# Moving the mask, the first two bias runs and half of the key copies of a neighbourhood-attention stage, with first scores two parts later

## The chip, the cores and the metric

The kernel runs on one core of one Trainium2 chip. The time is device microseconds (us) of one execution. The kernel before was timed in three runs: 1579.85, 1583.55 and 1585.72 us, median 1583.55 us. The profile used below is of one further execution of the same program.

A core has engines that run at the same time, each with its own ordered list of instructions: TensorE (PE in the profile; PEld is its loading of the stationary operand), VectorE (DVE), ScalarE (ACT), GpSimd (POOL) and SyncE (SP). SP computes nothing here: it issues DMA transfers. ACT issues transfers too, between its own computations; an instruction that has to wait holds up all that stand behind it on the same engine. In the profile, "SPq" and "ACTq" mark the issuing of a transfer.

## What is computed

The reference is one step of a small diffusion trunk of two layers, 512 latent tokens (8 rows of 64 columns) and 128 context tokens, width 1024, 16 heads of 64. The change lies in the first layer, whose token mixer is neighbourhood attention:

```
q, k, v = split(h @ w_qkv, 3)
s_lat = einsum(q, k[neighbouring rows]) * scale
s_lat = where(col_ok, s_lat + rpb[:, dr, dc], -inf)   # 2-D relative bias per head
s_ctx = einsum(q, k_ctx) * scale
p = softmax(concat(s_lat, s_ctx))
o = p_lat @ v + p_ctx @ v_ctx
```

A query of a latent token sees 16 neighbouring columns in all 8 rows, plus the 128 cached context keys. The context tokens attend only to themselves. After the mixer follow a projection, norms and a gated feed-forward block with a width-3 convolution; the second layer has grouped-query attention and the same feed-forward block. None of that is changed.

## The kernel before, in words

Weights arrive in f32. Each piece of 128x1024 is split into a high part, rounded to the matmul type (`wh`, by ACT, line 171), and the rest (`wl`, by VectorE or GpSimd, line 173); a product is three matmuls, high by high, high by low and low by high (`wsplit`, lines 166 to 180). The raw pieces `wr` are loaded by SP (line 169) into four buffers.

The beginning, up to about 52 us, loads and norms the tokens, makes the modulation and the transposed input `hT` (lines 580 to 582: ACT writes the high part, VectorE updates `xT` in place and then writes the low part), and computes the values of the first four heads (`v_part`; their copies out of PSUM are `na_v_put`, line 473). Its tiles lie in a pool that is given back at its end; the tiles of the attention stage (pool `na`, opened at line 760) are laid into the same memory, in the order of their first use, and an instruction that writes such a tile waits until the last reader of the old tile that lay there is done.

The attention stage works in pairs of heads. `na_qk_items(p)` gives for pair `p` two items: the queries and the keys, each of eight parts (two column halves, QKH, of four parts; a part is six matmuls, 128x256 in the first half and 128x384 in the second). When a half is complete, its result goes from PSUM to SBUF: for queries by lines 843 and 844, for keys by `k_put` (lines 813 to 818). `k_put` writes for each head `b` of the pair three things: the rounded key in the head's own half of the partitions (line 816, ACT), the same in the other half, "swapped" (line 817, ACT), and the rest `kl` (line 818, VectorE). The keys of the cached context come through a transpose (`tk`) and go the same way.

`na_table(h)` (lines 885 to 898) makes the bias table of a head: three transfers issued by ACT bring runs of the bias table from DRAM into the tile `tr` (one buffer; 128 rows of 996 bytes and two times 64 rows), and GpSimd subtracts them from the mask in three instructions (line 894) into one of two tiles `tb`. The mask itself is one transfer of 256 KB, issued by ACT at line 762. A second head's runs can only be fetched when the first head's table is done, because `tr` has one buffer.

`Head.scores(slot)` computes 128 queries against their 384 keys: two matmuls, VectorE adds the table and takes the minimum (line 929), ACT takes the exponential and its sum (line 933), VectorE the reciprocal (936), GpSimd scales (937). `turns` transposes the probabilities (`tp`), `values` multiplies with the values.

The order of the matmuls is written out by hand: `pe` (line 110) chains every TensorE instruction to the one before it, so TensorE works strictly in program order. `stream()` hands out the parts of all projections one by one through `fill`. At the start of the stage `fill(PRO)` takes PRO = 20 of them (16 of the first pair, 4 of the second pair's queries), then come the four score slots of head 0 with one part after each of the first three, and then, head by head, the lists ORDER0, ORDER and ORDER2, in which "f" is one more part, "s0" to "s3" are score slots of the next head and "t0" to "t2" are transposes. In all there are 173 such parts; after head 11 four early parts of the output projection (three matmuls of 128x512 each, `part0`) are put behind them, and head 12 uses up what is left.

On the other engines the order is not written out: a planner at build time lists instructions, by what it takes them to cost and to wait for. `behind(a, b)` (line 707) tells it that `a` has to stand after `b`; it adds no wait. There is one counter of completions for every eighth transfer, over both queues together, so that a transfer also waits for the one eight before it.

ACT keeps one table of functions at a time; the profile shows the loading of another one as ACT_TABLE_LOAD. The first of the stage's exponentials stands behind such a load.

Of the kernel before, what the change touches and what calls it, by code (L numbers as in the profile page):

```python
# [10 lines left out]
F32 = mybir.dt.float32  # L11
F32R = mybir.dt.float32r
BF16 = mybir.dt.bfloat16
AF = mybir.ActivationFunctionType
# [5 lines left out]
P = 128  # L20
D = 1024
# [13 lines left out]
RPAD = 32  # L35
RLEN = 15 * 31 + 2 * RPAD
RUN = 8 * 31 + 1
# [3 lines left out]
NPK = 6  # L41
# [14 lines left out]
    "t0 s0 s1 f f f t1 f f t2 f s2 f s3 f f f f f f f".split(),  # L56
    "p0 s0 s1 t0 f f f t1 f t2 f s2 p1 f s3 v p2 f f f f".split(),
)
PRO = 20
PSTEP = (3, 5, 6, 6, 8, 9)  # L60
WU = 29
TP = 1
# [10 lines left out]
def raw_ap(ap, offset, dims):  # L73
    return bass.AP(tensor=ap.tensor, offset=ap.offset + offset, ap=[list(d) for d in dims])
# [30 lines left out]
def hybrid_step(ctx: ExitStack, tc: tile.TileContext, A, O):  # L105
    nc = tc.nc
    no_sync = mybir.DependencyInfo(mybir.DependencyClass.NoSync, mybir.DependencyReason.DATA)
# [11 lines left out]
    def turn(*a, **k):  # L119
        pe(nc.tensor.transpose(*a, **k))  # L120

    def f32(t):
        return t.bitcast(F32)

# [37 lines left out]
    def x_in(t):  # L162
        return A["x_sample"][0, t * P : (t + 1) * P, :] if t < 4 else A["x_prompt"][0]


    def wsplit(src, a, b, low=None, own=None, pin=False, after=None):
        q = own or wp
        raw = wp.tile([P, a, b], F32, tag="wr", name="wr")
        nc.sync.dma_start(raw, src)
        hi = q.tile([P, a, b], F32R, tag="wh", name="wh")  # L170
        i = nc.scalar.copy(hi, raw)  # L171
        lo = q.tile([P, a, b], F32R, tag="wl", name="wl")
        j = (low or nc.vector).tensor_sub(lo, raw, f32(hi))  # L173
        if after:
            behind(i, after[0])
            behind(j, after[1])
        if pin:
            tc.keep_in_program_order(i)
            tc.keep_in_program_order(j)
        return hi, lo  # L180

    def rows(w, r0, nr, c0, ncol):
        return w[r0 * P : (r0 + nr) * P, c0 : c0 + ncol].rearrange("(k p) n -> p k n", p=P)
# [81 lines left out]
    def ada_work(p, rawp, group, steps, todo, wait=1, sizes=()):  # L265

        bias = p.tile([P, 256], F32, name="abias")
        gr = p.tile([P, 256], F32, name="again")  # L270
        nc.gpsimd.memset(bias, 0.0)
        nc.gpsimd.memset(gr, 0.0)

        def quarters(row):
            return row.rearrange("(j c) -> j c", j=4)

        loads = deque((l, idx, k) for l, idx in todo for k in range(KC))
        raws = deque()

        def load():  # L280
            if loads:
                l, idx, k = loads.popleft()
                raw = rawp.tile([P, D], F32, tag="wr", name="wr")
                nc.sync.dma_start(raw, A["ada_w"][l, k * P : k * P + P, idx * D : idx * D + D])
                raws.append((l, idx, k, raw))

        for _ in range(group):
            load()
        for _ in range(wait):
            yield  # L290
        sizes = iter(sizes)
        while raws:
            n = min(len(raws), next(sizes, len(raws)))
            for _ in range(n):
                l, idx, k, raw = raws.popleft()
                if k == 0:
                    for q in range(2):
                        nc.sync.dma_start(bias[q::32, :], quarters(A["ada_b"][l, idx * D : idx * D + D]))
                        if idx in gain_of:
                            nc.sync.dma_start(gr[q::32, :], quarters(A[gain_of[idx]][l]))  # L300
                    ps = bk.get("ada")
                for j in range(4):
                    mm(ps[32 * j : 32 * j + 32, 0:256], scolp[:, 2 * k : 2 * k + 32], raw[:, 256 * j : 256 * j + 256],
                       start=k == 0, stop=k == KC - 1)
                if k < KC - 1:
                    continue
                orow = p.tile([P, 256], F32, tag="arow", name="arow")
                nc.vector.tensor_add(orow, ps[:, 0:256], bias)
                bk.put(ps)
                if idx in gain_of:  # L310
                    nc.vector.scalar_tensor_tensor(
                        orow, orow, 1.0 if idx in (1, 4) else 0.0, gr, op0=ALU.add, op1=ALU.mult
                    )
                for q in range(2):
                    nc.scalar.dma_start(quarters(modrow[l][idx][q]), orow[q::32, :])
            for i in range(steps):
                for _ in range(n if steps == 1 else i < n):
                    load()
                yield
# [150 lines left out]
        return vpool.tile([P, 6, 4, HD], F32, tag="vt", name="vt", bufs=2)  # L470

    def na_v_put(vt, c, src):
        nc.scalar.copy(vt[:, c], src.rearrange("p (a d) -> p a d", a=4))

    def na_v_cache(vts, g):
        vc = vpool.tile([P, 256], F32, tag="vc", name="vc", bufs=1)
# [13 lines left out]
    with ExitStack() as s:  # L490
# [154 lines left out]
        v_part(6, range(NT))  # L645
        for c in range(NT):
            v_part(7, (c,))
            na_v_put(vts_of[0], c, vb[c][:, 0:256])
            if c == 4:
                na_v_out(0, vb[c][:, 0:256])  # L650
            bk.put(vb[c])

# [49 lines left out]
            nc.scalar.copy(hi, raw)  # L704
            return nc.vector.tensor_sub(lo, raw, f32(hi))

    def behind(ins, other):
        tc.add_manual_dep(ins.ins, other.ins.name, no_sync, reason="order")

    class Mix:  # L710


# [46 lines left out]
    with l_na:  # L759
        ap = l_na.enter_context(pool("na", 2))  # L760
        mask = ap.tile([P, 2, 32, 8], F32, name="mask", bufs=1)
        nc.scalar.dma_start(mask, A["k_mask"])
        tbs = [ap.tile([P, 7, P], F32, name=f"tb{i}", bufs=1) for i in range(2)]
        for tb in tbs:
            nc.gpsimd.memset(tb[:, 3, :], 0.0)
# [33 lines left out]
        def na_qk_items(p):  # L799
            d = {}  # L800
# [8 lines left out]

            def load_k():  # L810
                d["wk"] = wsplit(rows(wqkv, 0, 8, 1024 + P * p, P), 8, P, nc.gpsimd if p else None)

            def k_put(c0, c1, src):
                for b in range(2):
                    own, oth = own_oth(b)
                    nc.scalar.copy(d["kh"][b][own, c0:c1], src[own])
                    nc.scalar.copy(d["kh"][b][oth, c0:c1], src[own])
                    nc.vector.tensor_sub(d["kl"][b][own, c0:c1], src[own], f32(d["kh"][b][own, c0:c1]))

            def part(which, half, k0):  # L820
                w = d["w"] if which == 0 else d["wk"]
# [61 lines left out]
            return v6[:, 0:5:2, :] if slot == 0 else v6[:, slot - 1 : slot + 2, :]  # L883

        def na_table(h):
            tr = ap.tile([P, 2, RUN], F32, tag="tr", name="tr", bufs=1)
            base = h * RLEN + RPAD
            for dst, off, n in ((tr[:, 0, :], -8, 16), (tr[0:64, 1, :], 8, 8), (tr[64:128, 1, :], -16, 8)):
                nc.scalar.dma_start(dst, raw_ap(A["k_rpb"], base + off, [[1, n], [31, 8], [1, RUN]]))
            tb = tbs[h % 2]  # L890
            for w, dst in ((1, tb[:, 0::6, :]), (0, tb[:, 1:3, :]), (0, tb[:, 4:6, :])):
                t0 = tr[:, w, :]
                rv = raw_ap(t0, RUN - 1, [t0.ap[0], [-16, 2], [-1, 16], [-31, 8]])
                nc.gpsimd.tensor_sub(
                    dst.rearrange("p c (a b) -> p c a b", b=8),
                    mask[:, w].rearrange("p (c a) b -> p c a b", c=2), rv,
                )
            return tb
# [983 lines left out]
```

## Time and profile before

| | |
|---|---|
| median of three runs | 1583.55 us (1579.85 to 1585.72) |
| profiled execution, its own time | 1582.82 us |
| span of the profiled execution, first to last instruction | 1580.9 us |
| TensorE busy in the span | 1524.0 us, 96% |
| VectorE, ACT, GpSimd busy | 1024.6, 861.1, 701.9 us |
| mean granted TensorE clock | 0.99 |

The page of a profile and the views behind it name instructions by line, engine, operation and tile, as `out<-in`. In a view of the timeline each row gives the start, the duration, the engine, the line and the operation; in square brackets stands how long the engine was idle before it and what released it. A row of stages gives start and end, the length, the busy time of PE, PEld, DVE, ACT and POOL, the granted TensorE clock (1.00 is full) and the share of the DMA engines' time. The idle time of an engine costs something only where it ends up on the path that sets the end.

### The profile page before, as it was taken

How to read it: one execution, taken by the hardware profiler on the slowest of the kernel's cores; microseconds unless marked ns; L12 is line 12 of the kernel's file. 1: busy time of each engine (PE TensorE's matmuls, PEld its weight loads, DVE VectorE, ACT ScalarE, POOL GpSimd, SP SyncE). 2: the span in 40 equal slices, each digit the busy share in tenths (PEclk: the TensorE clock that was granted, in tenths of full speed). 3: DMA queues.
4: the chain of work that ended last, by engine and by line, in shares of the span. 5: the costliest groups of instructions: out<-in, count | busy, mean ns of one | idle time of the engine just before them, and what ended most of it. 6: DMA issues, size and time to landing. Idle time of an engine off the chain costs nothing.

```text
span 1580.9 us, 26049 instructions
## 1 busy us (share of the span) xinstructions
PE 1524.0 (96%) x9709; PEld 1349.4 (85%) x9709; DVE 1024.6 (65%) x1654; ACT 861.1 (54%) x1641; POOL 701.9 (44%) x605
## 2 busy tenths in 40 slices
PE   6799999999999999999999989999999999999998
PEld 4689899788999999988887767777899999998886
DVE  4353444649877666765746867773888888886554
ACT  4474655646655555554444536764656666554443
POOL 1455554332355455534443354541325556553433
PEclk9999999999999999999999998999999999999999
DMA  9845454244465666587573110003633334448664
GB/s 300 196 113 142 127 145 118 75 151 157 154 231 185 218 186 201 176 272 267 192 223 112 60 39 15 1 1 131 229 116 105 114 105 150 132 157 269 213 217 140
DMA packets 193210, 242.41 MB, mean 153 GB/s; under 512 B 11100, under 2 KB 149564, under 8 KB 193084
## 3 DMA queue, kind: packets, MB, share of 16 engines
q1 hardware_dynamic: 182224, 233.13, 46.0%
q10 hardware_dynamic: 10860, 7.62, 2.9%
q8 instruction: 76, 1.25, 0.3%
q14 instruction: 50, 0.41, 0.1%
HBM read 214.38 MB, written 26.34 MB: 152 GB/s over the span
## 4 chain that ended last, share of the span: by engine, by line
PE 58%; DVE 7%; ACT 3%; POOL 3%; issue 2%; DMA 2%; ACTq 0%; POOLq 0%; DVEq 0%
PE ux L117 17%; PE acc L117 16%; PE uz L117 8%; PE uy L117 4%; PE y L117 2%; PE po L117 2%; PE s L117 2%; PE gp L117 2%; PE tp L120 2%; PE ada L117 2%; DVE t L1244 1%; DMA wr<-in_ffn_w_up 1%; DMA wr<-in_ffn_w_down 1%; DVE wl L173 1%; POOL wl L173 1%
## 5 line engine op out<-in xcount | busy, mean ns | idle before, releaser
L173 POOL TENSOR_TENSOR wl<-wr,wh 128x1024 fp32r<-128x1024 f32 x70 | 172.2, 2464 | 237.4 <-ACT wh L171 226.5
L1167 POOL TENSOR_TENSOR wl<-wr,wh 128x1024 fp32r<-128x1024 f32 x76 | 183.5, 2436 | 47.3 <-ACT wh L1166 43.8
L117 PE MATMUL ux<-B,wh 128*128 128x322 f32 x832 | 200.0, 311 | 0.0
L1244 DVE SCALAR_TENSOR_TENSOR t<-C,cw,t 128x644 f32<-128x644 f32 x176 | 156.3, 888 | 51.3 <-ACT t L1242 50.7
L117 PE MATMUL acc<-wh,alo 128*128 128x512 f32 x440 | 172.3, 392 | 0.3 <-DVE alo L1136 0.3
L117 PE MATMUL acc<-wl,ahi 128*128 128x512 f32 x440 | 172.0, 391 | 0.3 <-POOL wl L173 0.3
L117 PE MATMUL acc<-wh,ahi 128*128 128x512 f32 x440 | 171.9, 391 | 0.0
L171 ACT CAST wh<-wr 128x1024 fp32r<-128x1024 f32 x140 | 145.0, 1048 | 45.1 <-DMA wr<-in_ffn_w_down 33.6
L117 PE MATMUL uz<-B,wh 128*128 128x322 f32 x640 | 156.3, 312 | 0.0
L117 PEld LDWEIGHTS ux<-B,wh 128*128 128x128 f32 x832 | 143.6, 189 | 2.1 <-issue 1.2
L1136 DVE TENSOR_TENSOR alo<-ain,ahi 128x384 fp32r<-128x384 f32 (+1 forms) x88 | 79.5, 923 | 87.7 <-ACT ahi L1134 86.7
L117 PE MATMUL ux<-B,wl 128*128 128x322 f32 x416 | 129.5, 311 | 2.7 <-DVE wl L1167 2.7
L117 PE MATMUL qk<-hT,wh 128*128 128x384 f32 (+1 forms) x512 | 123.4, 317 | 0.0
L117 PEld LDWEIGHTS uz<-B,wh 128*128 128x128 f32 x640 | 110.9, 189 | 3.7 <-issue 1.6
L1167 POOL TENSOR_TENSOR vl<-wr,vh 128x1024 fp32r<-128x1024 f32 x38 | 96.5, 2540 | 24.6 <-ACT vh L1166 24.3
L173 DVE TENSOR_TENSOR wl<-wr,wh 128x1024 fp32r<-128x1024 f32 x70 | 93.7, 1352 | 20.0 <-ACT wh L171 19.5
L1166 ACT CAST wh<-wr 128x1024 fp32r<-128x1024 f32 x84 | 84.9, 1049 | 39.3 <-DVE wr L1190 39.0
L1242 ACT ACTIVATE t<-C,cw 128x644 f32<-128x644 f32 x88 | 78.6, 893 | 47.9 <-DVE C L1272 40.3
L117 PE MATMUL uz<-B,wl 128*128 128x322 f32 x320 | 99.5, 311 | 0.3 <-POOL wl L1167 0.3
L117 PEld LDWEIGHTS acc<-wh,alo 128*128 128x128 f32 x440 | 82.6, 188 | 18.9 <-DVE alo L1136 1.1
L117 PEld LDWEIGHTS acc<-wl,ahi 128*128 128x128 f32 x440 | 82.6, 188 | 18.5 <-POOL wl L173 0.7
L117 PEld LDWEIGHTS acc<-wh,ahi 128*128 128x128 f32 x440 | 82.6, 188 | 17.7
(251 smaller groups left out, 3885.2 us busy)
## 6 DMA issues: line engine op xcount, KB each, us to landing
wr<-in_ffn_w_up SPq DMA_DIRECT2D x88, 512.0 KB
wr<-in_ffn_w_down SPq DMA_DIRECT2D x88, 512.0 KB
wr<-in_ada_w SPq DMA_DIRECT2D x80, 512.0 KB
act<-act SPq DMA_DIRECT2D x44, 321.0 KB
wr<-in_na_w_qkv SPq DMA_DIRECT2D x24, 512.0 KB
mod<-modrow SPq DMA_DIRECT2D x20, 512.0 KB
ain<-act SPq DMA_DIRECT2D x44, 192.0 KB
wf<-in_ada_w SPq DMA_DIRECT2D x16, 512.0 KB
```

The costliest lines, as they stand in the source:

```text
L117: pe(nc.tensor.matmul(*a, **k))
L120: pe(nc.tensor.transpose(*a, **k))
L171: i = nc.scalar.copy(hi, raw)
L173: j = (low or nc.vector).tensor_sub(lo, raw, f32(hi))
L1136: pin(nc.vector.tensor_sub(lo[:, 0 : c1 - c0], ain[:, 0 : c1 - c0], f32(hi[:, 0 : c1 - c0])))
L1166: nc.scalar.copy(hl[0], src)
L1167: low.tensor_sub(hl[1], src, f32(hl[0]))
L1242: nc.scalar.activation(t, taps(0), AF.Identity, bias=cw[:, 3, n : n + 1], scale=cw[:, 1, n : n + 1])
L1244: nc.vector.scalar_tensor_tensor(t, taps(d), cw[:, w, n : n + 1], t, op0=ALU.mult, op1=ALU.add)
```

## The change

- The mask and the runs of heads 0 and 1 are issued by SP instead of ACT, directly behind the load of the first pair's key weights (`load_k`). The runs of head 1 get a buffer of their own, out of the six of tag `pk`.
- The three loads by SP that follow in program order (`queue.extend([i] * 3)`; these are the weights of the second pair's queries and keys and the first piece of the modulation weights `ada_w`) are put behind the last of those transfers.
- The runs of head 2 stay in ACT's list; they are put behind the last copy of the first pair's keys by ACT (`kput`).
- The swapped key halves of the first pair (line 817) are written by VectorE instead of ACT.
- A small exponential of one column stands behind the last value copy of the first stage, so that the table of functions is loaded there.
- PRO goes from 20 to 22: two more parts run ahead of head 0's scores.

`behind` moves up in the file without a change. The diff:

```diff
-PRO = 20
+PRO = 22
...
+    queue = []
...
     def wsplit(src, a, b, low=None, own=None, pin=False, after=None):
         q = own or wp
         raw = wp.tile([P, a, b], F32, tag="wr", name="wr")
-        nc.sync.dma_start(raw, src)
+        i = nc.sync.dma_start(raw, src)
+        if queue:
+            behind(i, queue.pop())
...
                 raw = rawp.tile([P, D], F32, tag="wr", name="wr")
-                nc.sync.dma_start(raw, A["ada_w"][l, k * P : k * P + P, idx * D : idx * D + D])
+                i = nc.sync.dma_start(raw, A["ada_w"][l, k * P : k * P + P, idx * D : idx * D + D])
+                if queue:
+                    behind(i, queue.pop())
...
     def na_v_put(vt, c, src):
-        nc.scalar.copy(vt[:, c], src.rearrange("p (a d) -> p a d", a=4))
+        return nc.scalar.copy(vt[:, c], src.rearrange("p (a d) -> p a d", a=4))
...
-            na_v_put(vts_of[0], c, vb[c][:, 0:256])
+            i = na_v_put(vts_of[0], c, vb[c][:, 0:256])
...
+        behind(nc.scalar.activation(sm.tile([P, 1], F32, name="exp1"), mhalf, AF.Exp), i)
...
         mask = ap.tile([P, 2, 32, 8], F32, name="mask", bufs=1)
-        nc.scalar.dma_start(mask, A["k_mask"])
+        runs, kput = {}, []
+
+        def na_runs(h, q=nc.scalar):
+            if h == 1:
+                tr = ap.tile([P, 512], F32, tag="pk", name="tr1", bufs=NPK)[:, 0 : 2 * RUN]
+                tr = tr.rearrange("p (a b) -> p a b", a=2)
+            else:
+                tr = ap.tile([P, 2, RUN], F32, tag="tr", name="tr", bufs=1)
+            runs[h] = tr
+            base = h * RLEN + RPAD
+            for dst, off, n in ((tr[:, 0, :], -8, 16), (tr[0:64, 1, :], 8, 8), (tr[64:128, 1, :], -16, 8)):
+                i = q.dma_start(dst, raw_ap(A["k_rpb"], base + off, [[1, n], [31, 8], [1, RUN]]))
+                if h == 2:
+                    behind(i, kput[0])
+            return i
...
             def load_k():
                 d["wk"] = wsplit(rows(wqkv, 0, 8, 1024 + P * p, P), 8, P, nc.gpsimd if p else None)
+                if not p:
+                    nc.sync.dma_start(mask, A["k_mask"])
+                    for h in range(2):
+                        i = na_runs(h, nc.sync)
+                    queue.extend([i] * 3)
...
                     own, oth = own_oth(b)
-                    nc.scalar.copy(d["kh"][b][own, c0:c1], src[own])
-                    nc.scalar.copy(d["kh"][b][oth, c0:c1], src[own])
+                    i = nc.scalar.copy(d["kh"][b][own, c0:c1], src[own])
+                    (nc.scalar.copy if p else nc.vector.tensor_copy)(d["kh"][b][oth, c0:c1], src[own])
                     nc.vector.tensor_sub(d["kl"][b][own, c0:c1], src[own], f32(d["kh"][b][own, c0:c1]))
+                if not p:
+                    kput[:] = [i]
...
         def na_table(h):
-            tr = ap.tile([P, 2, RUN], F32, tag="tr", name="tr", bufs=1)
-            base = h * RLEN + RPAD
-            for dst, off, n in ((tr[:, 0, :], -8, 16), (tr[0:64, 1, :], 8, 8), (tr[64:128, 1, :], -16, 8)):
-                nc.scalar.dma_start(dst, raw_ap(A["k_rpb"], base + off, [[1, n], [31, 8], [1, RUN]]))
+            if h not in runs:
+                na_runs(h)
+            tr = runs.pop(h)
```

More of the change, by code (lines that the diff above doesn't have):

```diff
@@ L120, in turn, with behind @@
         pe(nc.tensor.transpose(*a, **k))
+    def behind(ins, other):
+        tc.add_manual_dep(ins.ins, other.ins.name, no_sync, reason="order")
     def f32(t):
@@ L705, in split @@
             return nc.vector.tensor_sub(lo, raw, f32(hi))
-    def behind(ins, other):
-        tc.add_manual_dep(ins.ins, other.ins.name, no_sync, reason="order")
     class Mix:
```

## The prediction

> **What bounds the kernel now.** I read the page first, then the timeline of TensorE for its longest idle time, then a table of stages around it, then the timelines of the engines that it points to.
>
> ```profile
> span 1580.9 us, 26049 instructions
> PE 1524.0 (96%) x9709; PEld 1349.4 (85%) x9709; DVE 1024.6 (65%) x1654; ACT 861.1 (54%) x1641; POOL 701.9 (44%) x605
> ...
> 69.47 0.28 PE L117 MATMUL qk<-hT,wl 128*128 128x256 f32 x1
> 69.59 0.28 PE L117 MATMUL qk<-hT,wh 128*128 128x256 f32 x1
> 79.36 0.69 PE L117 MATMUL s<-kh,qs 128*128 128x384 f32 x1 [9.49 <-ACT kh L817]
> ...
> 60.00:69.90 9.90, 9.87 (x72) 9.66 (x70) 1.11 (x2) 1.91 (x3) 2.79 (x4) 1.00 0.64 145
> 69.90:79.30 9.40, 0.00 (x0) 0.00 (x0) 1.87 (x6) 4.35 (x14) 4.59 (x4) 0.70 0.61 99
> 79.40:83.80 4.40, 4.40 (x13) 4.01 (x14) 2.47 (x6) 4.29 (x8) 3.20 (x2) 0.50 0.17 26
> 83.90:90.00 6.10, 6.08 (x41) 5.85 (x40) 3.14 (x13) 4.54 (x12) 4.77 (x7) 1.00 0.37 107
> ...
> 100.00:280.00 180.00, 179.25 (x1414) 162.89 (x1414) 75.75 (x227) 104.81 (x288) 93.84 (x96) 1.00 0.50 130
> 280.00:310.00 30.00, 27.97 (x185) 24.10 (x182) 20.82 (x52) 21.42 (x56) 13.52 (x15) 1.00 0.25 64
> ```
>
> TensorE is busy for 96% of the span, and its order is fixed, so each of its holes costs its whole length. One hole stands out: part 20 is done at 69.87, and the first score matmul starts at 79.36, after 9.49 us without any matmul, waiting for a swapped key half (line 817). The rows of stages show a second price: from 79.40 to 83.80 the granted clock is 0.50. It is 1.00 again in the row from 83.90. So 4.4 us of matmuls take twice their time, 2.2 us lost. Afterwards TensorE is full: 179.25 of 180 us. The hole with its tail is worth 9.49 + 2.2 = 11.7 us, 0.74% of the time. Nothing else that the change touches has TensorE waiting.
>
> Why the keys are late, from ACT's timeline:
>
> ```profile
> 55.67 0.38 ACT L843 ACTIVATE qs<-qk 64x256 fp32r<-64x256 f32 x1 [2.26 <-PE qk L117]
> 57.01 0.38 ACT L843 ACTIVATE qs<-qk 64x256 fp32r<-64x256 f32 x1
> 59.56 2.08 ACTq L889 DMA_DIRECT2D tr<-in_k_rpb  x3
> 61.73 1.29 ACTq L477 DMA_DIRECT2D vc<-in_cache_na_v  x1
> 63.08 0.48 ACT L843 ACTIVATE qs<-qk 64x384 fp32r<-64x384 f32 x1 [5.69 <-DMA tr<-in_k_rpb]
> ...
> 69.71 1.24 ACTq L889 DMA_DIRECT2D tr<-in_k_rpb  x2
> 71.00 0.22 ACT L843 ACTIVATE qs<-qk 64x64 fp32r<-64x64 f32 x1 [5.98 <-issue]
> ...
> 76.30 1.84 ACTq L889 DMA_DIRECT2D tr<-in_k_rpb  x3
> 78.19 0.27 ACT L858 COPY kp<-qk 128x128 f32<-128x128 f32 x1 [3.35 <-issue]
> 78.83 0.47 ACT L817 CAST kh<-qk 64x384 fp32r<-64x384 f32 x1
> ...
> 81.78 1.28 ACT L933 ACT_TABLE_LOAD   x1
> ```
>
> ACT stands still three times, for 5.69 + 5.98 + 3.35 = 15.0 us, each time with a bias transfer at the head of its list: head 0's runs, then head 1's, which need the one `tr` buffer, then head 2's, which need it again. The table rows of GpSimd, with two of its earlier ones and one of VectorE that are used further down, show the other end: the buffer is freed at 69.68 and again at 76.27, and the next issue follows within 0.03 us.
>
> ```profile
> 49.61 0.81 DVE L582 TENSOR_TENSOR hT<-xT,hT 128x640 fp32r<-128x640 f32 x1
> ...
> 50.57 0.35 POOL L765 MEMSET tb<- 128x128 f32 x2 [32.67 <-DVE hT L582]
> ...
> 57.07 2.39 POOL L173 TENSOR_TENSOR wl<-wr,wh 128x1024 fp32r<-128x1024 f32 x1 [0.16 <-ACT wh L171]
> 65.10 1.70 POOL L894 TENSOR_TENSOR tb<-mask,tr 128x256 f32<-128x256 f32 x2 [5.65 <-DMA tr<-in_k_rpb]
> 68.81 0.87 POOL L894 TENSOR_TENSOR tb<-mask,tr 128x256 f32<-128x256 f32 x1 [2.01 <-DMA tr<-in_k_rpb]
> ...
> 75.42 0.85 POOL L894 TENSOR_TENSOR tb<-mask,tr 128x256 f32<-128x256 f32 x1 [0.68 <-DVE kl L818]
> ```
>
> **The change part by part.** *Transfers off ACT, a buffer for head 1.* Seven issues leave ACT: 2.08 us for three of the runs' issues and 1.24 for two, 3.9 with the sixth (the mask's left out), and with them the first two stalls. The third goes because head 2's issues are put behind the last key copy. The Trainium skill, "DMA: Bandwidth & Descriptors", rules for kernel authors, says that spreading transfers over the issuing engines buys no bandwidth and saves only issue time. By that rule alone the move is worth the 3.9 us of issuing, against 15.0 us by the rows, since here the issuing engine was held by a buffer; the trace decides. The rule's case, a hole shorter by 3.9 alone, would end at 1582.82 - 3.9 = 1578.9, and is counted below with the smaller hole.
>
> *When the keys are ready then.* The last part of the first pair's keys leaves TensorE as the second pair's start:
>
> ```profile
> 66.97 0.27 PE L117 MATMUL qk<-hT,wl 128*128 128x256 f32 x1
> ...
> 86.13 0.34 PE L117 MATMUL s<-kl,qs 128*128 128x384 f32 x1
> 86.31 0.33 PE L117 MATMUL qk<-hT,wh 128*128 128x384 f32 x1
> ...
> 63.59 0.55 DVE L844 SCALAR_TENSOR_TENSOR qs<-qk,qs 64x384 fp32r<-64x384 f32 x1 [5.75 <-ACT qs L843]
> ```
>
> From 66.97 ACT needs 0.27 + 2 x 0.47 = 1.2 us (it no longer writes line 817). VectorE gets the swapped copies. Its price for them is not in the trace. Near rows are 0.55 us (line 844, 64x384, also out of PSUM) above and ACT's 0.47 for the very copy below; I take 0.55. With two `kl` of 0.55 this is 2.2 us, so the last key is there at 66.97 + 0.27 + 0.47 + 2.2 = 69.9, and head 0's own a bit earlier. VectorE had 1.11 us of work in the 9.9 us before, so nothing queues there.
>
> *PRO 22.* Two more parts, the first two of 128x384. By the start-to-start of such rows (0.18 us, 86.13 to 86.31) a part of six takes 1.05 to 1.1, so scores begin at 69.87 + 2.1 = 72.0, 2.1 us after the keys. Parts are only moved, so they cost nothing here; what they were cover for comes below. Hole zero; 11.7 us gained.
>
> *Function table ahead.* 1.28 us move from between score and probability to about 53, where ACT idles until 55.67 for the queries. Cost nothing; if that cover were gone, 1.5 us of ACT, which has 2 us of room before 72. No matmul waited for it, so no gain either.
>
> *What goes behind SP's transfers.* This is the part that could hurt. SP now issues the first key weights, the mask, six run transfers, and only then the second pair's query weights. By shapes the mask (2 KB per partition), the tables (7 KB), `kl` (12 KB) and the cached keys (1 KB) fill 22 KB before `tr`, and the earlier stage has one `x0` (4 KB) and then `xT` (20 KB): `tr` lies on `xT`'s end. The memset row above waited for the same release, line 582's last at 50.42. So the runs cannot be issued before 50.4, and SP stands there, with all that is behind it.
>
> ```profile
> 41.53 3.53 SPq L169 DMA_DIRECT2D wr<-in_na_w_qkv  x2
> ...
> 373.90 5.48 DMA wr<-in_ffn_w_up
> ...
> 79.33 1.04 ACT L171 CAST wh<-wr 128x1024 fp32r<-128x1024 f32 x1
> ```
>
> Before, the second pair's query weights were issued at 41.53. Now: six issues at 0.62 (1.24 for two) from 50.4 end at 54.1; a 512 KB load takes 5.48 us in the only row of the chain that shows one, so it is there at 59.6; ACT's cast 1.04 and GpSimd's rest 2.39 end at 63.0. TensorE wants it at 66.97: 4 us to spare, and cost nothing. From the other side: a set of runs took 5.7 us from first issue to its third table (69.71 to 75.42) with the queue to itself, and 9.25 us (59.56 to 68.81) beside two weight loads. Two sets one after the other before the weights start would be 11.4 or 18.5 us: weights split at 50.4 + 11.4 + 5.48 + 3.43 = 70.7, or at 77.8, a new hole of 3.7 or 10.9 us. I take the overlapped value, because transfers of one list overlap in the rows (three issued in 1.8 us landed within one set's time), and the loads that slowed head 0's set now stand behind it. Both ends stay for the range. The second pair's keys are wanted another 6 parts later and come 0.4 us behind.
>
> *What comes late next.* Two parts run ahead are two parts fewer in head 12, after whose last scores stand the four early parts as cover:
>
> ```profile
> 298.19 0.48 PE L117 MATMUL y<-wh,oh 128*128 128x512 f32 x1
> 300.84 0.39 PE L117 MATMUL y<-wh,ol 128*128 128x512 f32 x1
> 304.32 0.33 PE L120 MATMUL tp<-ident,p 128*128 128x128 f32 x1 [0.87 <-POOL p L937]
> ...
> 88.10 1.15 POOL L937 TENSOR_SCALAR p<-p,rc 128x384 f32<-128x384 f32 x2
> 88.80 0.84 PE L120 MATMUL tp<-ident,p 128*128 128x128 f32 x4
> ```
>
> The four take 3.0 us, and TensorE already waits 0.87 for the probabilities behind them. With two left the wait grows by 1.5. In head 0, from the last score's end (86.47) to its scaled probabilities (89.25) 2.8 us pass, and the three parts between are now all of 128x256 (0.12 us a matmul, 69.47 to 69.59), 2.2 us instead of 2.5: 0.4 us more, rounded up, taken whole, at full clock.
>
> **Sum**, against the profiled execution's 1582.82: -9.49 - 2.2 + 1.5 + 0.4 = -9.8, so 1573.0. That execution lies 0.7 below the median of the runs, so on the median's footing it is 1573 to 1574; I say 1573, since I rounded the small losses up.
>
> **The rivals.** *A smaller hole stays* (1578). The runs take the uncontended 5.7 us each in turn, and the second pair's query weights are 3.7 us late at 66.97; a hole of that length is where the clock falls, another 1.7. -9.8 + 3.7 + 1.7 = -4.4. For it: SP is held until 50.4. Against: 4 us of room. The Trainium skill, "TensorE: Matmul & The Clock Gate", part 1, puts the fall to half clock after one idle window of about 3.4 us; the 0.70 and 0.50 of the stages agree, and by that rule a hole below it would cost only itself, 1576.
>
> *The time is given back later* (1582). The other engines would then be the bound once TensorE comes 11.7 us earlier. For it: the load of 5.48 us stands on the chain at 373.90. Against: in 100 to 280 ACT is busy 104.81 and GpSimd 93.84 of 180, and that load starts when the splits in front of it free its buffer, so it moves along.
>
> *The weights come far too late* (1586, slower). One mechanism at SP: the runs take the contended 9.25 us a set, in turn, and the query weights of the second pair are split at 77.8. -9.8 + 10.9 + 2.2 (clock) = +3.3. It decides from a hole of 7.6 us (9.8 less the clock's 2.2) on, when these weights land after 66.97 + 7.6 - 3.43 = 71.1. For it: head 0's set did take that long. Against: beside loads which now come later.
>
> *The change doesn't do it* (1583). The planner could put ACT's copies behind another waiting instruction, the cast of weights that now land later above all. It would have to be held until after 70.
>
> **How the numbers follow.** Forecast 0.62, smaller hole 0.17, given back or not done 0.14, slower 0.07. The low end is the full 11.7 with nothing given back, 1571.1, less the 3.0 by which the runs before reach below the profiled one: 1568. The high end takes in the smaller hole and most of no change: 1583. A measurement of this kernel tells about 0.5% (7.9 us) from no change: faster means below 1575.6. That is nearly all of the forecast and little of the rest, 0.60; slower, above 1591.5, only a bad tail of the last rivals, 0.04; the same 0.36.
>
> **What would show it.** Right: no idle TensorE over 1 us between 60 and 90, granted clock 1.00 there, scores at about 72, ACT with no wait in front of a transfer of `tr`, the three tables of head 0 before 62, the table load near 53, and head 12's wait grown to about 2.4 us. Wrong: a hole before the second pair's parts released by `wl` of GpSimd or `wh` of ACT, with the load's landing in front of it; or the hole gone and the end not earlier.

## The result, and the profile after

The kernel after takes 1609.9 us (median of five runs, 1607.2 to 1611.65); the kernel before, on the same chip, takes 1583.55 us. The ratio is 1.0168, 95% interval 1.0151 to 1.0185: slower, by some 26 us. The forecast was 1573.0, with a range up to 1583.

In the kernel after, code below line 160 stands 5 to 29 lines further down: the cast `wh` is line 178, the key copies are 843 to 845, the table is line 922, the exponential 961, the scaling 965.

The profiled execution spans 1605.1 us (before: 1580.9), of which TensorE is busy for 1535.5 (before: 1524.0).

Rows of stages (start and end, length, busy time of PE, PEld, DVE, ACT and POOL with their counts, granted clock, share of the DMA engines, GB/s):

```profile
71.60:75.00 3.40, 0.00 (x0) 0.00 (x0) 2.75 (x10) 2.50 (x8) 1.01 (x2) 0.99 0.86 259
75.00:78.30 3.30, 3.22 (x11) 3.22 (x12) 2.67 (x6) 1.82 (x4) 3.30 (x2) 0.50 0.11 32
...
100.00:280.00 180.00, 170.05 (x1295) 153.74 (x1292) 71.83 (x215) 98.80 (x273) 86.94 (x88) 0.97 0.45 123
```

The hole at the start is shorter (3.4 us in place of 9.4), but it is not the only one any more. The stretch from 100 to 280, which held 179.25 us of matmuls in 180 before, now holds 170.05, at a clock of 0.97. TensorE's timeline shows the longer holes one by one:

```profile
75.08 0.48 PE L120 MATMUL tk<-ident,kp 128*128 128x128 f32 x1 [3.48 <-ACT kp L887]
...
89.38 0.47 PE L120 MATMUL tp<-ident,p 128*128 128x128 f32 x1 [3.35 <-POOL p L965]
...
116.25 1.09 PE L120 MATMUL tp<-ident,pp 128*128 128x128 f32 x4 [3.04 <-POOL p L965]
...
187.90 1.09 PE L120 MATMUL tp<-ident,pp 128*128 128x128 f32 x4 [3.18 <-POOL p L965]
...
258.81 0.68 PE L120 MATMUL tp<-ident,pp 128*128 128x128 f32 x4 [3.16 <-POOL p L965]
...
315.12 0.33 PE L120 MATMUL tk<-ident,kp 128*128 128x128 f32 x1 [2.72 <-ACT kp L887]
...
322.84 0.33 PE L120 MATMUL tp<-ident,p 128*128 128x128 f32 x1 [2.08 <-POOL p L965]
...
324.62 0.47 PE L120 MATMUL tp<-ident,p 128*128 128x128 f32 x1 [1.45 <-POOL p L965]
```

Three kinds are new: three times some 3.1 us in front of the transposes of the prompt's probabilities (`pp`; the prompt is the 128 context tokens, whose own attention is worked off in heads 1, 5, 9 and 13; the holes are in the first three), a group at head 0's transposes (85 to 91), and a group at the end of the stage (312 to 325). The first matmul behind the stage (`ux`, the first number behind the last comma) tells how much of the loss lies in the stage; before, then after:

```profile
L117 PE MATMUL ux<-B,wh x832: 303/310/416, 372.0 to 1417.3; 128*128 128x322 f32 x167
```

```profile
L117 PE MATMUL ux<-B,wh x832: 304/310/416, 393.5 to 1439.1; 128*128 128x322 f32 x167
```

21.5 of the 24.2 us between the spans. The stretch behind it took between 1208.9 us (before; after: 1211.6) and 1215.6 us in the profiles of this study. The kernel before has the shortest; the others, from 1211.4 on, follow no order that the edits would explain. So a single span tells no better than some 3 us, and the medians are used below.

### The profile page after: what moved, and what is told of

Same layout as the page of the kernel before. It is cut to its first block, busy times and chain, and to the rows that moved or that the text cites. A ratio compares the mean times of both kernels' runs of the same rounds, so it can differ in the third digit from the quotient of the medians.

```text
span 1605.1 us, 26048 instructions
## 1 busy us (share of the span) xinstructions
PE 1535.5 (96%) x9709; PEld 1357.3 (85%) x9709; DVE 1026.2 (64%) x1660; ACT 858.9 (54%) x1636; POOL 702.9 (44%) x605
## 4 chain that ended last, share of the span: by engine, by line
PE 58%; DVE 8%; ACT 3%; POOL 3%; issue 2%; DMA 1%; ACTq 0%; POOLq 0%; DVEq 0%
PE acc L117 18%; PE ux L117 17%; PE uz L117 7%; PE uy L117 4%; PE y L117 2%; PE s L117 2%; PE po L117 2%; PE tp L120 2%; PE ada L117 2%; DVE t L1272 1%; POOL rh L1518 1%; DMA wr<-in_ffn_w_up 1%; DVE wl L180 1%; DMA gn<-in_gqa_k_norm 1%; ACT junk L368 1%
## 5 line engine op out<-in xcount | busy, mean ns | idle before, releaser
L117 PE MATMUL qk<-hT,wh 128*128 128x384 f32 (+1 forms) x512 | 128.6, 326 | 0.0
```

The costliest lines, as they stand in the source:

```text
L117: pe(nc.tensor.matmul(*a, **k))
```

## The experiments

**Which part costs the time.** Two kernels: the one after with 20 parts ahead, and the one before with 22.

```diff
-PRO = 22
+PRO = 20
```

> The change with PRO back at 20, all else kept. Phase theory (the two parts moved ahead shift all later parts against the lists of the heads, and that costs in heads 1, 5, 9 and 12): the three holes of 3.0 to 3.2 us in front of the prompt's transposes (113, 185 and 256 us) are gone, and the time is below the kernel before, 1570 to 1578. Transfer theory (the moved transfers, copies and the planner's new order cost it): 1600 to 1612, the three holes stay.

Measured: 1586.25 us, ratio to before 1.0015 (1.0006 to 1.0025). The hole in front of the first scores is 4.92 us, `ux` starts at 372.1, and the three holes at `pp` are gone:

```profile
76.54 0.69 PE L117 MATMUL s<-kh,qs 128*128 128x384 f32 x1 [4.92 <-DVE kh L844]
```

The phase theory is right about the holes, but its 1570 to 1578 is missed by 8 us.

```diff
-PRO = 20
+PRO = 22
```

(in the kernel before)

> The kernel before with PRO 22 alone. Phase theory: the three holes of about 3 us with about 1.5 us of half clock each appear in front of the prompt's transposes (+14), head 12 loses some 6, and the hole in front of head 0's scores is still there: 1597 to 1606. Transfer theory: 1581 to 1586, at most 2 us away from the kernel before.

Measured: 1609.68 us, ratio 1.0154 (1.0132 to 1.0177). This is the phase theory again, though longer than its 1597 to 1606. So the two parts are the whole loss, 24 to 26 us, and all the rest of the change together brings nothing where 11.7 us were expected (9.8 with the two parts). That leaves two questions: what the two parts cost, and where the gain went.

**The two parts: banks.** The program hands out the banks of PSUM, the memory that matmuls write to, from a list, the one given back first first: a ring. The transposes of `pp` read nothing but `pp`, which GpSimd has done at 112.4; the scaling that the profile of the kernel after names as releaser (line 965) writes another tile. In the kernel before with 22 parts the first of the three holes is put down to VectorE's second half of a query eviction (there line 844), and in the kernel after that instruction ends at 116.10, 0.15 us before the transposes start. TensorE of the kernel before with 22 parts, then GpSimd of the kernel after, then its VectorE:

```profile
117.47 0.73 PE L120 MATMUL tp<-ident,pp 128*128 128x128 f32 x4 [3.01 <-DVE qs L844]
```

```profile
111.33 1.05 POOL L687 TENSOR_TENSOR pp<-pp,rcp 128x512 f32<-128x512 f32 x1 [4.74 <-DVE rcp L686]
```

```profile
115.87 0.23 DVE L873 SCALAR_TENSOR_TENSOR qs<-qk,qs 64x64 fp32r<-64x64 f32 x1
```

The theory: two parts more turn the ring of banks, so that the prompt's transposes get the bank of a query part that has just ended, where with 20 parts they got one that was long free. The run turns the ring by one place ahead of each such transpose:

```diff
                 if pr and step == "p1":
+                    bk.free.rotate(-1)
                     pth = prompt_turn(ap, pp, "pk", NPK)
```

> The changed kernel with the list of free PSUM banks turned by one place just before the prompt's transposes in heads 1, 5, 9 and 13, so that these take a bank last read by the copy of transposed probabilities and not the bank of the query part that VectorE still reads. Bank theory (TensorE waits for the bank, not for the probabilities pp or the scaling that the profile names): the holes at 113, 185 and 256 us shrink below 0.8 us and the time falls by 10 to 14, to 1596 to 1600. If TensorE waits for GpSimd there: holes stay, 1607 to 1612.

Measured: 1594.99 us, ratio 1.0065 (1.0046 to 1.0083), 15 us under the kernel after. What TensorE waited for between 90 and 290 us (in total, times, longest), after and with the ring turned:

```profile
PE tp L120 <- POOL p L965: 10.3, 4, 3.2
```

```profile
PE tp L120 <- ACT pk L978: 1.4, 3, 0.5
```

The sum agrees with the trace: 3.04 + 3.18 + 3.16 us of holes, and behind each one window of 3.4 us at half clock (1.7 lost), 14.5 us; less the 1.4 us of new waits, the stage should end 13.1 us sooner, and it ends 12.8 sooner (`ux` at 380.7). TensorE waited there for a bank, not for a value.

**The tail at the start.** With 22 parts the transpose of the first pair's cached keys for output (`tail`, put behind the second pair's fifth part) falls among the parts ahead of the first scores; the hole of 3.48 us stands in front of it. The run puts it two parts later:

```diff
-                    if i == 4 and tail:
+                    if i == (4 if n > 2 else 6) and tail:
```

> The changed kernel with the transpose of the first two pairs' key output (tk out of kp) two parts later, which for the first pair puts it behind head 0's first scores again. If that transpose alone makes the hole at 71.6 us: the hole goes and the time falls by 3 to 5, to 1605 to 1607. If the keys themselves are late: the scores now wait in its place, within 1 us of the same length, and the time stays at 1608 to 1611.

Measured: 1608.06 us, ratio 1.0147 (1.013 to 1.0164). The hole only moves, to 2.67 us in front of the first score:

```profile
74.49 0.44 PE L117 MATMUL s<-kh,qs 128*128 128x384 f32 x1 [2.67 <-DVE kh L844]
```

So the keys themselves are still late. ACT's timeline of the kernel after says why:

```profile
53.46 1.28 ACT L661 ACT_TABLE_LOAD   x1
...
55.83 0.36 ACTq L494 DMA_DIRECT2D out_new_na_v<-vo  x1
56.24 0.38 ACT L872 ACTIVATE qs<-qk 64x256 fp32r<-64x256 f32 x1 [1.28 <-DMA kc<-in_cache_na_k]
...
63.58 0.33 ACTq L486 DMA_DIRECT2D vc<-in_cache_na_v  x1
63.95 1.05 ACT L178 CAST wh<-wr 128x1024 fp32r<-128x1024 f32 x1 [6.48 <-DMA out_new_na_v<-vo]
68.21 0.41 ACT L482 COPY vt<-vc 128x256 f32<-128x256 f32 x1 [3.20 <-DMA vc<-in_cache_na_v]
...
69.59 0.48 ACT L872 ACTIVATE qs<-qk 64x384 fp32r<-64x384 f32 x1
...
76.84 0.47 ACT L843 CAST kh<-qk 64x384 fp32r<-64x384 f32 x1 [0.49 <-DVE kl L845]
```

The waits in front of transfers of `tr` are gone, as forecast. In their place ACT stands 6.48 us in front of the transfer of the next values (`vc`, line 486), which needs a buffer that the store of `vo` still holds, and 3.20 us for its landing. Behind these stand the cast of weights and, at 69.59, the query eviction and all key copies. The store of `vo` is issued at 55.83, and the instruction that waits for it goes on at 63.6. SyncE's timeline of the kernel after (start, then the time that the row's issues took together) and two rows of its stages show what the store met:

```profile
43.13 0.34 SPq L835 DMA_DIRECT2D mask<-in_k_mask  x1
50.51 3.89 SPq L780 DMA_DIRECT2D tr<-in_k_rpb  x6
54.45 1.08 SPq L174 DMA_DIRECT2D wr<-in_na_w_qkv  x2
56.50 3.78 SPq L291 DMA_DIRECT2D wr<-in_ada_w  x2
```

```profile
43.00:50.50 7.50, 7.39 (x67) 6.80 (x68) 3.90 (x12) 4.77 (x7) 0.00 (x0) 1.00 0.56 128
...
54.50:63.60 9.10, 9.10 (x65) 9.10 (x64) 0.84 (x2) 1.20 (x4) 5.16 (x7) 1.00 0.95 249
```

The kernel before in the same stages:

```profile
43.00:50.50 7.50, 7.42 (x67) 6.83 (x68) 3.76 (x11) 4.88 (x8) 0.00 (x0) 1.00 1.18 288
...
54.50:63.60 9.10, 9.10 (x65) 9.10 (x64) 0.85 (x3) 2.22 (x5) 4.80 (x4) 1.00 0.69 154
```

From the mask's issue at 43.13 to 50.51 SyncE stands in front of the first run, whose tile is not free, and four weight loads stand behind it: they go out from 54.45 on, in the kernel before from 41.53 on. From 43.0 to 50.5 the DMA engines move 128 GB/s in place of 288; 160 GB/s less in 7.5 us is 1.2 MB, which then runs from 54.5 on together with the runs and the store.

**Where the gain went: four runs with two theories.** First, `vc`'s transfer put behind the last key copy, at 20 parts:

```diff
     def na_v_cache(vts, g):
...
-        nc.scalar.dma_start(
+        i = nc.scalar.dma_start(
...
+        if g == 1:
+            behind(i, kput[0])
...
```

> The changed kernel with the prompt's parts back at 20, and with the second head group's transfer of cached values (L486) issued by ScalarE only after its last copy of the first pair's keys. Theory: the keys are late because ScalarE stands for about 5 us in front of that transfer, which waits for the shared buffer vc to be free (its last store lands late behind the tables), and about 4 us more in front of vt<-vc. Then the hole of 4.92 us in front of the first scores falls below 1.5 us, the half clock window with it, and the time goes from 1586.3 to 1576 to 1581 us. Rival: the casts of the late query weights hold the keys as well, so the hole only falls to 3 to 4 us: 1583 to 1587. Second rival: the cached values, now late themselves, open a new wait in head 0's last turn: 1585 to 1590.

Measured: 1581.9 us, ratio 0.9992 (0.9983 to 1.0001); 4.4 us under the same kernel without this edit. The hole shrinks from 4.92 to 1.49 us:

```profile
70.98 0.44 PE L117 MATMUL s<-kh,qs 128*128 128x384 f32 x1 [1.49 <-DVE kh L846]
```

So ACT's wait for `vc` was most of it; the rest is probably the casts of late weights (ACT waits 4.11 and 0.97 us for `wr` there), which this run alone does not show. The time can't be told from that of the kernel before, although the stage ends 6.0 us sooner (`ux` at 366.0).

Second, the six runs and the mask without the rule that put the weight loads behind them:

```diff
                     for h in range(2):
                         i = na_runs(h, nc.sync)
-                    queue.extend([i] * 3)
```

> The changed kernel with the prompt's parts back at 20, and with the six transfers of the first two heads' runs and the mask behind all four of the second pair's weight transfers in SyncE's queue, instead of behind one of them. Theory (tables crowd the transfers between 54 and 63 us): the query weights and the store that frees vc land 3 to 5 us sooner, ScalarE's wait in front of L486 falls from 5.0 to 1 to 2 us, the hole to 0 to 2 us, and the time to 1577 to 1582 us; the tables of head 0 are then late by 2 to 4 us but not wanted before about 76. Rival (the store is late for another cause, or the tables are now what the first sum waits for): the hole stays at 4 to 6 us, 1584 to 1590.

Measured: 1577.87 us, ratio 0.9963 (0.995 to 0.9977). SyncE of this kernel, a row of its stages, and ACT:

```profile
41.13 3.46 SPq L174 DMA_DIRECT2D wr<-in_na_w_qkv  x2
44.64 2.20 SPq L291 DMA_DIRECT2D wr<-in_ada_w  x2
...
50.02 4.14 SPq L780 DMA_DIRECT2D tr<-in_k_rpb  x6
```

```profile
43.00:50.50 7.50, 7.50 (x71) 7.10 (x64) 4.19 (x12) 5.30 (x8) 0.35 (x2) 1.00 1.17 290
```

```profile
53.01 0.38 ACTq L494 DMA_DIRECT2D out_new_na_v<-vo  x1
...
57.34 0.34 ACTq L486 DMA_DIRECT2D vc<-in_cache_na_v  x1
59.43 0.49 ACT L871 ACTIVATE qs<-qk 64x384 fp32r<-64x384 f32 x1 [2.39 <-PE qk L117]
```

TensorE's first score, and the first `ux`:

```profile
69.29 0.34 PE L117 MATMUL s<-kh,qs 128*128 128x384 f32 x1
```

```profile
L117 PE MATMUL ux<-B,wh x832: 304/310/416, 361.7 to 1409.8; 128*128 128x322 f32 x167
```

The runs still start at 50.02, when their tile is free, but the weights now go in front of them. The store of `vo` goes at 53.01 in place of 55.83 in the kernel after, where ACT had first loaded the function table and done the small exponential (53.46 to 54.96) and then stood for the landing of cached keys (the wait of 1.28 us above); how much of the gain is this and how much the emptier DMA engines, the run doesn't separate. `vc` is issued at 57.34 in place of 63.58, ACT takes the query eviction at 59.43 in place of 69.59, the first score runs at 69.29 without a hole, and the stage ends at 361.7, 10.3 us before the kernel before. (With 20 parts and the rule in place, store, `vc` and eviction were at 56.67, 63.26 and 69.85.) Of these 10.3 us only 5.7 are in the time: 1577.87 against 1583.57 of the kernel before. By these profiles some 4 us are lost again behind the stage; where, no run separates.

Third, both edits together:

> Both edits of the two runs before together, prompt's parts at 20. Theory: no hole over 1 us in front of the first scores, no half clock before 85 us: 1573 to 1579 us, 5 to 10 us under the kernel before. Rival (the start waits for something else, the mask or the first tables): a hole of 3 us or more at the first sum or its transposes, 1581 to 1587.

Measured: 1579.53 us, ratio 0.9969 (0.996 to 0.9979). No hole in front of the scores either, but 1.85 us at head 0's transposes, where ACT now waits 0.93 us for `vc` among the exponentials and two tables stand between the scalings on GpSimd. With the weights first, moving `vc` brings nothing.

Fourth, `vc` behind the keys at 22 parts with the ring turned:

> The changed kernel (prompt's parts at 22) with the cached values' transfer behind the key copies and with the ring of banks turned by one place ahead of each prompt turn. Theory: the hole at 71.6 us falls from 3.5 us to below 1.5 us, the three holes of 3 us at the prompt's transposes stay away, and what is left is the end of the stage: 1587 to 1592 us, against 1595 with the ring turned alone. Rival (the start's hole costs nothing at 22 parts, since the parts behind it are only moved): 1593 to 1597.

Measured: 1592.87 us, ratio 1.0055 (1.004 to 1.007). The hole at 71.6 is gone, but holes of 2.9 and 3.3 us stand at head 0's transposes; 2 us less than with the ring alone. The numbers fit neither expectation well: what is gained in front of the scores is waited for behind them.

**What the other two parts of the change are worth.** With the weights first in the queue and 20 parts, first the swapped copies back on ACT, then the function table loaded where it is wanted as well:

```diff
-                    (nc.scalar.copy if p else nc.vector.tensor_copy)(d["kh"][b][oth, c0:c1], src[own])
+                    nc.scalar.copy(d["kh"][b][oth, c0:c1], src[own])
```

> The run with 20 parts and the weights first in SyncE's queue, with the first pair's swapped key copies on ScalarE again as before the change. There the last key copy ended at 68.93 us and the first score matmul started at 69.29 without a hole. Theory (the transfers, not the copies, held the keys): two more copies of 0.47 us on ScalarE make the keys 0.9 to 1.5 us later, a hole of at most 1.2 us, below any half clock: 0 to 1.5 us over that run's 1577.9, so 1578 to 1580. Rival (half of the gain came from VectorE's share): a hole over 2 us, 1581 to 1584.

```diff
-        behind(nc.scalar.activation(sm.tile([P, 1], F32, name="exp1"), mhalf, AF.Exp), i)
```

> As the run beside it (copies on ScalarE, weights first in SyncE's queue, 20 parts), and the function table loaded again where the first probabilities want it. So only the mask, the first two heads' runs, their issuer and head 1's buffer differ from the kernel before. Theory: the load of 1.28 us lies between the first score and its probabilities, with three parts of cover, so at most 1.3 us: 1578 to 1581, still 3 to 5 us under the kernel before. Rival (the table ahead is what spares the wait of the first transposes): a wait of 2 to 3 us in front of tp<-p near 78 us, 1581 to 1584.

Measured: 1576.74 us, ratio 0.9967 (0.9954 to 0.9979), and 1575.22 us, ratio 0.9948 (0.9935 to 0.9962), against 1577.87 (0.995 to 0.9977) with both. Neither part brings anything, and the intervals overlap. In the last of the three the table is loaded late and in the open, but at a place where no matmul waits for it:

```profile
72.35 1.28 ACT L959 ACT_TABLE_LOAD   x1
```

Its median is the lowest of the study, 8 us under the kernel before. What is left in it of the change is the mask and the runs of two heads on SyncE behind the weights, a buffer for head 1, and head 2's runs behind the last key copy. Which of these gives how much, no run separates.

**What is left of the two parts.** With the weights first, 22 parts and the ring turned, and then with two parts given back in head 10, so that the stage's end has its cover again:

> The weights first in SyncE's queue, as in the best run so far, but with 22 parts ahead as in the changed kernel and the ring of banks turned by one place ahead of each prompt turn. Theory: no hole at the start and none at the prompt's transposes, so that what is left against 20 parts is the end of the stage (holes of 2.7, 2.1 and 1.5 us with a half clock between): 6 to 9 us over 1577.9, so 1584 to 1587. Rival (22 parts cost nothing but the bank): 1577 to 1580.

```diff
-                    if i < len(order) - 1 or h % 4 or not h:
+                    if (i < len(order) - 1 or h % 4 or not h) and not (h == 10 and i > len(order) - 3):
```

> As the run beside it, with the two parts given back late: head 10 takes its last two parts out of its order, so that from there on the stage stands as with 20 parts (no turn of the ring at head 13). Theory (the end of the stage lacks the cover of two parts): the holes near 300 to 310 us shrink to those of 20 parts, 0.9 us each, and the time falls to 1577 to 1580. Rival (they come from the tail or the bank, not from the missing cover): 1584 to 1587 as the run beside it; or head 10 itself lacks the two parts and waits instead.

Measured: 1587.65 us, ratio 1.0029 (1.0017 to 1.0041), and 1582.68 us, ratio 1.0001 (0.9992 to 1.001). (The second also leaves out the turn of the ring at head 13.) The first is 9.8 us over the same kernel with 20 parts; giving the two parts back takes 5.0 of them. The end of the stage, without and with it:

```profile
294.13 0.33 PE L120 MATMUL tk<-ident,kp 128*128 128x128 f32 x1 [2.70 <-ACT kp L886]
...
304.00 0.33 PE L120 MATMUL tp<-ident,p 128*128 128x128 f32 x1 [1.45 <-POOL p L964]
```

```profile
296.16 0.33 PE L120 MATMUL tk<-ident,kp 128*128 128x128 f32 x1 [0.19 <-ACT kp L886]
```

The last pair's `tail` had no score slot left between itself and the part that feeds it; that is the larger piece, and not the one that had been forecast. The one forecast came as priced: head 12's wait is 0.90 + 1.45 us in the first run and 0.87 in the second, 1.5 more. The other 5 us are the theory's miss: at 22 parts head 0's transposes wait longer, 2.52 + 1.05 us where they waited 1.05 with 20. GpSimd of the run without the two parts given back shows the queue:

```profile
74.91 0.90 POOL L921 TENSOR_TENSOR tb<-mask,tr 128x256 f32<-128x256 f32 x1 [4.42 <-DMA tr<-in_k_rpb]
75.80 1.16 POOL L964 TENSOR_SCALAR p<-p,rc 128x384 f32<-128x384 f32 x2
...
77.75 2.35 POOL L180 TENSOR_TENSOR wl<-wr,wh 128x1024 fp32r<-128x1024 f32 x1
80.07 0.59 POOL L964 TENSOR_SCALAR p<-p,rc 128x384 f32<-128x384 f32 x1
```

The planner has put a split of 2.35 us, and tables that wait for head 2's runs, between head 0's scalings. The last run takes these scalings off GpSimd:

```diff
-                nc.gpsimd.tensor_scalar(pt, pt, rc[:, slot : slot + 1], 1.0, op0=ALU.mult, op1=ALU.mult)
+                (nc.gpsimd if self.h else nc.vector).tensor_scalar(pt, pt, rc[:, slot : slot + 1], 1.0, op0=ALU.mult, op1=ALU.mult)
```

> As the run with 22 parts, weights first, ring turned and two parts given back (1582.7 us), with head 0's probabilities scaled by VectorE instead of GpSimd, whose order puts them behind head 1's first tables, a table of head 2 that waits 4.4 us for its runs, and a split of 2.4 us. Theory (what 22 parts still cost is this queue in front of head 0's transposes: holes of 2.0 and 0.9 us and half a clock window of 6.8 us): the holes in front of tp<-p near 80 us fall below 0.6 us, no half clock before 100 us, 1577.5 to 1580. Rival (the transposes wait for something else that comes with 22 parts, the last score or its exponential): the holes stay over 2 us in sum, 1582 to 1584.

Measured: 1581.12 us, ratio 0.9983 (0.9973 to 0.9992). The holes shrink from 2.04 + 0.91 to 0.97 + 0.91 us and the time by 1.6 us, with intervals that just touch: a part of it, less than the theory asked for. The remaining 3 us to the kernel with 20 parts were not separated by a run; the trace has for them a half-clock window and waits of 0.5 to 0.8 us up to head 9.

## Why the prediction was wrong

**The step that failed** is the one named PRO 22, with "Parts are only moved, so they cost nothing here", and its continuation under what comes late next, priced at 1.5 + 0.4 us. Measured: 23.7 us (20 against 22 in the kernel after). 15 us of it is the turned ring of banks, which the prediction did not look at; 5.0 (measured with the weights first) the stage's end, where the forecast had 1.5 for head 12's probabilities, which came, and missed the tail with its 2.72; some 5 more go mostly to head 0's transposes, priced 0.4, which waited 0.72 + 0.24 + 3.35 + 0.91 us in the kernel after and 0.80 + 0.23 + 1.05 with 20 parts: 3.1 us more, and behind the 3.35 a stretch at half clock that the kernel with 20 parts doesn't have there. These pieces come from different kernels and need not add up exactly. The price at head 0 was worked out from TensorE's cover alone; what stands between the scalings on GpSimd was not read.

**The second step that failed** is the queue behind SyncE. The prediction had SyncE standing until 50.4 with all that is behind it, and that came: issues from 50.51 to 54.40, the second pair's query weights issued at 54.45, and TensorE waited 0.4 us for them in the end. The 4 us of room were used up: the low part of these weights was ready at 67.5, where the forecast had 63.0. But only these weights were followed. Four loads stood still for 7 us, and their bytes came down on the store of `vo`, on whose buffer ACT's list depended. So of the term -9.49 - 2.2 nothing was left at the end of the stage (`ux` at 372.1 with 20 parts, 372.0 before): the hole only shrank to 4.92 us, half clock stood behind it as before, new waits of 0.80 + 0.23 + 1.05 us came at head 0's transposes, and in that profile the parts ahead of the scores ended 1.7 us later than before (71.62 against 69.87), a difference whose cause no run shows. This is the rival "the change doesn't do it", with another waiting instruction in front than the one it thought of most, and "until after 70" as it said: ACT's last key copy ends at 77.3. Its price, 1583, is near the 1586.25 of the kernel with 20 parts.

**What held.** The hole's price within the stage: with it and the half clock gone (weights first, 20 parts) the stage ended 10.3 us earlier, 11.7 had been counted, and 1.05 us are left at head 0's transposes. At the end of the kernel 5.7 of it arrived in that kernel and 8.0 in the one with the lowest median; the rival "the time is given back later" had a part in it, though no run shows by what. ACT's stalls in front of `tr`: gone. Head 0's tables were done before 62, as foretold: those of both heads by 60.95. VectorE's price for the swapped copies: 0.55 us for 64x384, as taken; but their place on the path was wrong, as with the weights first the same copies on ACT made no difference. The table load: 1.28 us at 53.46, no gain, and with the weights first no cost; in the kernel after it stood in front of the store of `vo`, and what that cost there, no run shows. The rival of weights far too late did not come (its hole of 10.9 us is 10.8 by its own terms, which changes nothing).

On the Trainium skill's rule that spreading transfers over issuing engines saves only issue time ("DMA: Bandwidth & Descriptors", rules for kernel authors): the run with the lowest median moves the mask and two heads' runs to another issuer, with a buffer for head 1 and head 2's runs placed later, and gains 8.0 us. That is more than the 3.9 of issuing, as the prediction had argued from the held buffer. The kernel after shows the other half: on SyncE the same transfers held other loads.

## What to carry to other kernels

Moving a step by a few places in a fixed order also turns every ring that it draws from: read which buffer or bank each later step then gets, and who used it last; otherwise a wait can appear that no data explains. When an issue is put into a queue, ask from when its tile is free; everything behind it stands until then, and what it delays comes down on something else. And where one engine's list holds several waits in a row, removing the first shows the second: take the landing times of all of them before counting the gain.

## What the runs showed of the hardware

The clock fell after much shorter holes than the prediction assumed. In the kernel with `vc` put behind the keys, rows of stages:

```profile
69.50:70.90 1.40, 0.00 (x0) 0.00 (x0) 1.35 (x3) 1.40 (x3) 1.40 (x1) 1.00 0.80 268
...
72.20:75.40 3.20, 3.20 (x12) 3.11 (x12) 2.72 (x8) 1.08 (x3) 1.62 (x1) 0.50 0.85 207
```

A hole of 1.49 us was followed by 3.4 us at half clock; behind one of 1.05 us in the kernel with the weights first and 20 parts the clock stayed at 1.00. Length alone does not decide: behind the 2.72 us at the end of the stage in the kernel after it stayed, too:

```profile
315.20:318.50 3.30, 3.30 (x16) 2.85 (x17) 3.23 (x6) 3.17 (x7) 2.10 (x2) 1.00 0.90 273
```

The Trainium skill, "TensorE: Matmul & The Clock Gate", part 1, asks for an idle window of about 3.4 us; the prediction's rival drew 1576 from that, and these rows do not bear it out: half clock also came where the idle time was 1.49 us.

In the last run VectorE's scaling, 0.41 us at other places, took 2.02 us beside GpSimd's split; VectorE, then GpSimd:

```profile
75.69 0.41 DVE L964 TENSOR_SCALAR p<-p,rc 128x384 f32<-128x384 f32 x1
...
77.38 2.02 DVE L964 TENSOR_SCALAR p<-p,rc 128x384 f32<-128x384 f32 x1
```

```profile
76.81 2.37 POOL L180 TENSOR_TENSOR wl<-wr,wh 128x1024 fp32r<-128x1024 f32 x1
```

It ended at 79.40, 0.22 us after the split. The Trainium skill, "SBUF — State Buffer", the section on the two separate sides, has it that the two engines share a pair of ports, and that a GpSimd instruction which starts first holds them for its whole length against a VectorE instruction in a two-port mode or with two inputs from SBUF. The rows fit that: of head 0's four scalings only this one started while GpSimd was at work. It does not hold for every VectorE instruction: a query eviction at 79.43 took its usual 0.56 us beside a table instruction of GpSimd. One of the scalings moved from GpSimd to VectorE to spare a wait thus waited for GpSimd all the same.
